# Two blocks on one core: a weight unit's low part made on GpSimd or on the vector engine

## The chip, the cores and the metric

The kernel runs on one core of a Trainium2 chip. Of the core's engines it uses TensorE (PE in the profile; its weight loads are PEld), the vector engine (DVE), ScalarE (ACT), GpSimd (POOL) and the DMA queues, most of them issued by SyncE (SP). The metric is the device time of one execution in microseconds (us). Three runs of the kernel before the change gave 1938.38, 1938.04 and 1938.17 us, median 1938.17. One more execution was profiled: it took 1938.33 us, and its profile spans 1936.6 us.

## What is computed

Activations of 256 tokens by 1024 features pass through two blocks, each of two layers. A layer is a feed-forward part, a mixer and a second feed-forward part, all with residual additions:

```
x = x + 0.5 * norm(swiglu(norm(x), w_gu, w_down))
x = x + norm(mixer(norm(x)))
x = x + 0.5 * norm(swiglu(norm(x), w_gu, w_down))
```

In the first block the mixer joins three paths: a gated linear recurrence with a short causal convolution of four taps, a chunked state-space path with such a convolution too, and a gated spatial unit. In the second block the mixer is a retention and a latent attention. All is float32, and nearly all of the arithmetic is products of the activations with weight matrices that are read from HBM once: 341 MB go through the main DMA queue.

## The kernel before, in words

**Products in three passes.** A float32 product is made from rounded parts. Each operand is split into a high part in the fast matmul format (`fp32r`) and a low part, the rest. `mm3` issues three matmuls into one accumulator: high by high, high activation by low weight, low activation by high weight. The 256 tokens are two tiles (t = 0 and 1) of 128, and each weight is used by both.

**Weight units.** `_plan` cuts all weights into 658 units of 128 rows by up to 1024 columns in the order of their use. Three processes prepare them: `loader` issues a DMA from SP into one of 6 `raw` buffers; `split_hi` makes the high part `whi` (a cast on DVE or ACT) into one of 9 buffers; `split_lo` makes the low part `wlo` = raw - high into one of 9 buffers (line 702), then gives the raw buffer back and tells the matmuls that the unit is ready. Units whose rows are scaled by a gain (line 704) take another operation. A unit's high and low buffers come free when both tiles have used it.

**The order.** Nothing of the order is written by hand. `program` is a set of processes (generators) that yield one engine operation after another. The class `Sched` runs them on a model of the engines, in which `Engine.make` (line 323) gives each operation a duration, and takes at each step the most urgent of those that could begin first; the urgency is the length of the chain of work behind a step, from the last of six trials, plus a table of constants. `Either` (line 291) holds one operation in two forms for two engines, and `choose` (line 454) takes the engine on which it would end first in the model, with 0.3 us against DVE. The instructions are then issued in that order on each engine, and on the chip semaphores alone hold them back: an engine never takes a later instruction first. Where PE has nothing to do in the model, `filler` puts matmuls on a constant tile (`warm`, line 595) there.

**GpSimd before** makes 48 small powers, of one to three columns (`rs`, `rsyo`, `rsyl`, `rsyv`, `rsyb`: reciprocal roots for the norms), masks (`AFFINE_SELECT`), and issues a few DMAs. Every one of its operations counts as 0.85 us in the model (line 347).

**Names that matter.** `acc` and `tmp` are PSUM tiles; `raw`, `whi`, `wlo`, `big`, `scr`, `keep`, `xTh`, `xTl` lie in SBUF. In the first block's mixers the convolutions are the `SCALAR_TENSOR_TENSOR` rows `big<-big,fm` and `big<-scr,fm,big`. Operations recorded by the model's `issue` (line 469) all show L469.

Of the kernel before, what the change touches and what calls it, by code (L numbers as in the profile page):

```python
# [17 lines left out]
ALU = mybir.AluOpType  # L18
# [105 lines left out]
def _width(u):  # L124
    return len(u[0]) * sum(c[3] - c[2] for c in u[1])
# [83 lines left out]
class Blank:  # L209


    def __getattr__(self, name):
        return self
# [94 lines left out]
def size(ap):  # L308
    n = 1
    for d in ap.shape[1:]:  # L310
        n *= d
    return n
# [6 lines left out]
class Engine:  # L319
# [3 lines left out]
    def __getattr__(self, name):  # L323
        f = getattr(self.real, name)

        def make(out, *a, **k):
            n = size(out)
            lat, func = 0.13, None
            if self.key == "PE":
                lat = 0.2  # L330
                if name == "transpose":
                    dur = 0.109
                elif a[0].dtype == F32R:
                    dur = max(0.107, n / 2400.0) + 0.0143
                else:
                    dur = 0.223
            elif self.key == "ACT":
                dur = (0.052 if a[0].space == PSUM else 0.093) + n * 0.000833
                if "accum_out" in k:
                    dur += 0.05  # L340
                for q in ("scale", "bias", "accum_out"):
                    if q in k and not isinstance(k[q], (int, float)):
                        dur += 0.093
                if name == "activation" and a[1] in TABLES:
                    func = a[1]
            elif self.key == "POOL":
                dur, lat = 0.85, 0.25
            else:
                if name in ("tensor_reduce", "bn_stats"):
                    n = size(a[0])  # L350
                dur = 0.07 + n * 0.00104
                if name == "reciprocal":
                    dur = 0.07 + n * 0.00625
                elif name in ("tensor_copy", "tensor_scalar", "tensor_single_scalar") and a[0].space != PSUM:
                    dur = 0.07 + n * 0.00052
                if name in ("scalar_tensor_tensor", "tensor_scalar") and not isinstance(a[1], (int, float)):
                    dur += 0.06
            op = Op(self.key, f, (out,) + a, k, dur, lat, func)
            op.small = self.key == "PE" and (name == "transpose" or a[0].dtype != F32R)
            op.first = name == "transpose" or k.get("start", False)  # L360
            return op

        return make
# [189 lines left out]
def program(S, nc, pool, psp, x, wst, pfm, prow, post, lnp, mats, ret_dec, inv, pos, out):  # L553
    V, A, G, T = Engine("DVE", nc.vector), Engine("ACT", nc.scalar), nc.gpsimd, Engine("PE", nc.tensor)
    R = Engine("POOL", nc.gpsimd)
# [95 lines left out]
    raws, his, los = {}, {}, {}  # L651

    def gain(u):
        name, l, k = u[2]
        return fmc(name, l)[:, k:k + 1]
# [38 lines left out]
    def split_lo():  # L694
        for i, u in enumerate(units):
            yield hi_ev[i]
            yield from S.take(lo_pool, True)
            w = _width(u)
            los[i] = pool.tile([P, 1024], F32R, tag="wlo", name="wlo", bufs=NLO, align_bytes=256)
            h = his[i][:, :w].bitcast(F32)  # L700
            if u[2] is None:
                yield V.tensor_tensor(los[i][:, :w], raws[i][:, :w], h, op=ALU.subtract)
            else:
                yield V.scalar_tensor_tensor(los[i][:, :w], raws[i][:, :w], gain(u), h, op0=ALU.mult, op1=ALU.subtract)
            S.release(raw_pool)
            S.fire(w_ev[i])
# [1015 lines left out]
    S.spawn(loader())  # L1722
    S.spawn(split_hi())
    S.spawn(split_lo())
    ends = [S.spawn(thread(t)) for t in range(2)]
    S.spawn(prologue())
# [75 lines left out]
```

## Time and profile before

| | |
|---|---|
| median of 3 runs | 1938.17 us (1938.04 to 1938.38) |
| profiled execution, its own time | 1938.33 us |
| its span | 1936.6 us |
| PE busy | 1925.4 us (99%), 9247 matmuls |
| DVE busy | 1494.3 us (77%), 2385 instructions |
| of it wlo without a gain | 765.3 us, 638 instructions |
| ACT busy | 626.9 us (32%) |
| POOL busy | 52.9 us (3%), 76 instructions |
| DMA, main queue | 341.26 MB, 54.3% of the 16 engines' span |

The span is the time from the first to the last instruction; 1.7 us of the execution lie around it. Busy time is the time in which at least one instruction of the engine was under way. A row of a timeline reads: start, length, engine, line, operation, output<-inputs, shape, and in brackets the engine's idle time before it with what ended that. "x3" means three instructions in a row. A row's length covers an instruction from start to end, and the next may start before that end, so the difference of two starts is the time that one really takes from its engine.

### The profile page before, as it was taken

How to read it: one execution, taken by the hardware profiler on the slowest of the kernel's cores; microseconds unless marked ns; L12 is line 12 of the kernel's file. 1: busy time of each engine (PE TensorE's matmuls, PEld its weight loads, DVE VectorE, ACT ScalarE, POOL GpSimd, SP SyncE). 2: the span in 40 equal slices, each digit the busy share in tenths (PEclk: the TensorE clock that was granted, in tenths of full speed). 3: DMA queues.
4: the chain of work that ended last, by engine and by line, in shares of the span. 5: the costliest groups of instructions: out<-in, count | busy, mean ns of one | idle time of the engine just before them, and what ended most of it. 6: DMA issues, size and time to landing. Idle time of an engine off the chain costs nothing.

```text
span 1936.6 us, 24594 instructions
## 1 busy us (share of the span) xinstructions
PE 1925.4 (99%) x9247; PEld 1612.1 (83%) x9247; DVE 1494.3 (77%) x2385; ACT 626.9 (32%) x1136; POOL 52.9 (3%) x76
## 2 busy tenths in 40 slices
PE   9999999999999999999999999999999999999999
PEld 7888988888888898888888888888888888888887
DVE  7977898767767799776777779877777777987774
ACT  5211774211321287320232036631022102662220
POOL 1000010000000001000000000000000000000000
PEclk9999999999999999999999999999999999999999
DMA  8555546555655554654655554356565655545572
GB/s 317 179 191 177 166 148 196 195 167 194 224 177 182 180 168 145 199 190 163 208 186 183 185 180 155 125 178 184 180 203 174 184 181 184 159 126 170 178 217 65
DMA packets 98390, 346.89 MB, mean 179 GB/s; under 512 B 11424, under 2 KB 11680, under 8 KB 98272
## 3 DMA queue, kind: packets, MB, share of 16 engines
q1 hardware_dynamic: 97040, 341.26, 54.3%
q0 software_dynamic: 1088, 4.06, 0.6%
q8 instruction: 72, 1.18, 0.3%
q14 instruction: 46, 0.38, 0.1%
q10 hardware_dynamic: 144, 0.00, 0.0%
HBM read 344.24 MB, written 1.05 MB: 178 GB/s over the span
## 4 chain that ended last, share of the span: by engine, by line
PE 96%; ACT 2%; DVE 1%; POOL 0%; issue 0%; POOLq 0%
PE acc L469 89%; PE tmp L469 7%; ACT big L469 1%; ACT L469 1%; POOL rsyo L469 0%; PE tmp L595 0%; DVE wlo L469 0%; DVE x L469 0%; ACT whi L469 0%; DVE whi L469 0%; DVE big L469 0%; DVE scr L469 0%; ACT scr L469 0%; ACT xTh L469 0%; DVE rswo L469 0%
## 5 line engine op out<-in xcount | busy, mean ns | idle before, releaser
L469 DVE TENSOR_TENSOR wlo<-raw,whi 128x1024 fp32r<-128x1024 f32 (+4 forms) x638 | 765.3, 1201 | 56.1 <-ACT whi L469 43.1
L469 PE MATMUL acc<-whi,xTh 128*128 128x512 f32 (+3 forms) x1888 | 745.1, 395 | 0.0
L469 PE MATMUL acc<-wlo,xTh 128*128 128x512 f32 (+3 forms) x1888 | 729.5, 386 | 1.0 <-DVE wlo L469 1.0
L469 PE MATMUL acc<-whi,xTl 128*128 128x512 f32 (+3 forms) x1888 | 730.0, 387 | 0.0
L469 DVE CAST whi<-raw 128x1024 fp32r<-128x1024 f32 (+1 forms) x402 | 278.4, 692 | 260.7 <-PE acc L469 250.7
L469 PE MATMUL acc<-whi,big 128*128 128x512 f32 x1408 | 457.8, 392 | 0.0
L469 PEld LDWEIGHTS acc<-whi,xTl 128*128 128x128 f32 x1888 | 354.6, 188 | 69.7
L469 PEld LDWEIGHTS acc<-wlo,xTh 128*128 128x128 f32 x1888 | 355.4, 188 | 66.1 <-DVE wlo L469 3.7
L469 PEld LDWEIGHTS acc<-whi,xTh 128*128 128x128 f32 x1888 | 355.0, 188 | 63.8 <-ACT big L469 0.4
L469 ACT CAST whi<-raw 128x1024 fp32r<-128x1024 f32 (+4 forms) x236 | 235.1, 1004 | 303.3 <-PE acc L469 283.7
L469 PEld LDWEIGHTS acc<-whi,big 128*128 128x128 f32 x1408 | 264.5, 188 | 54.0
L469 PE MATMUL acc<-wlo,big 128*128 128x512 f32 x704 | 274.7, 390 | 0.0
L469 ACT ACTIVATE scr<-acc,rs 128x512 f32<-128x512 f32 (+3 forms) x123 | 79.9, 650 | 482.0 <-PE acc L469 477.7
L469 PEld LDWEIGHTS acc<-wlo,big 128*128 128x128 f32 x704 | 132.4, 188 | 26.6 <-DVE wlo L469 0.6
L469 DVE SCALAR_TENSOR_TENSOR scr<-acc,rs,scr 128x512 f32<-128x512 f32 (+1 forms) x96 | 67.3, 705 | 42.0 <-PE acc L469 36.1
L469 ACT CAST big<-tmp 128x512 fp32r<-128x512 f32 (+1 forms) x88 | 47.4, 546 | 158.2 <-PE tmp L469 157.8
L469 PE MATMUL tmp<-ident,scr 128*128 128x128 f32 x484 | 78.4, 273 | 0.1
L469 PEld LDWEIGHTS tmp<-ident,scr 128*128 128x128 f32 x484 | 59.9, 140 | 17.2 <-DVE scr L469 2.9
L469 DVE SCALAR_TENSOR_TENSOR xTl<-tmp,fm,xTh 128x128 fp32r<-128x128 f32 x192 | 58.0, 344 | 13.8 <-ACT xTh L469 12.3
L469 ACT ACTIVATE scr<-acc 128x512 f32<-128x512 f32 x24 | 14.2, 596 | 167.2 <-DVE scr L469 167.2
L469 ACT ACTIVATE xTh<-tmp,fm 128x128 fp32r<-128x128 f32 x167 | 53.3, 365 | 44.9 <-DVE xTl L469 23.7
L469 DVE TENSOR_TENSOR big<-tmp,big 128x512 fp32r<-128x512 f32 (+2 forms) x104 | 64.2, 633 | 3.5 <-ACT big L469 2.8
(222 smaller groups left out, 946.0 us busy)
## 6 DMA issues: line engine op xcount, KB each, us to landing
raw<-in_wst_dram SPq DMA_DIRECT2D x606, 512.0 KB, 3.6
raw<-in_wst_dram SPq DMA_DIRECT2D x28, 384.0 KB, 3.1
raw<-in_wst_dram SPq DMA_DIRECT2D x8, 416.0 KB, 3.1
raw<-in_wst_dram SPq DMA_DIRECT2D x8, 390.0 KB, 3.2
pg<-in_post_dram POOLq DMA_DIRECT2D x5, 512.0 KB, 3.9
raw<-in_wst_dram SPq DMA_DIRECT2D x8, 256.0 KB, 4.7
x<-in_x_dram SPq DMA_DIRECT2D x4, 256.0 KB, 4.9
out_dram<-x SPq DMA_DIRECT2D x4, 256.0 KB, 2.0
```

The costliest lines, as they stand in the source:

```text
L469: op.f(*op.a, **op.k)
```

## The change

`split_lo` may now take the low part of a unit without gain on either engine: the same subtraction is offered on DVE and on GpSimd, and `choose` picks one. The model's duration of a GpSimd operation of four columns or more becomes 0.1 us + 0.0019 us a column (768 columns count as 1.56 us and 1024 as 2.05 us); smaller ones keep 0.85 us.

```diff
@@ Engine.make
             elif self.key == "POOL":
-                dur, lat = 0.85, 0.25
+                dur, lat = 0.85 if n < 4 else 0.1 + n * 0.0019, 0.25
@@ split_lo
             if u[2] is None:
-                yield V.tensor_tensor(los[i][:, :w], raws[i][:, :w], h, op=ALU.subtract)
+                yield Either(*(e.tensor_tensor(los[i][:, :w], raws[i][:, :w], h, op=ALU.subtract) for e in (V, R)))
```

In the new order 61 of the 658 low parts are made on POOL, 36 of them 1024 columns wide, 21 of 768 or 780 and 4 of 512. Four are among the first six units of the program, 17 lie in the mixer of the first block's first layer and 18 in that of its second, and 22 are spread over the rest. As the model's times differ, the order changes on all engines. Of the filler matmuls on PE, 57 of 256 columns become 39, and 2 of 128 columns become 10.

**POOL in the first layer's mixer.** `rsyo`, `rs`, `rsyv` and `rsyb` are the small powers, the last number before the arrow tells them apart; `pg` is a DMA of gains. Before:

```order
L469 TENSOR_TENSOR rs_0_1677<-rsw_0_1762,mhalf 128x1
L469 TENSOR_TENSOR rsyo_1_1865<-rswo_1_1863,mhalf 128x1
L469 TENSOR_TENSOR rs_1_1840<-rsw_1_1905,mhalf 128x1
L469 TENSOR_TENSOR rsyv_0_2434<-rswv_0_2432,mhalf 128x1
L902 DMA pg<-in_post_dram 128x1024
L469 TENSOR_TENSOR rsyv_1_2578<-rswv_1_2576,mhalf 128x1
L469 TENSOR_TENSOR rsyb_0_2748<-rswb_0_2746,mhalf 128x1
L469 TENSOR_TENSOR rsyb_1_2876<-rswb_1_2874,mhalf 128x1
```

The same place now:

```order
L469 TENSOR_TENSOR rs_1_1840<-rsw_1_1907,mhalf 128x1
L469 TENSOR_TENSOR wlo<-raw,whi 128x780 x2
L469 TENSOR_TENSOR wlo<-raw,whi 128x768 x2
L469 TENSOR_TENSOR wlo<-raw,whi 128x1024 x3
L469 TENSOR_TENSOR wlo<-raw,whi 128x768 x4
L469 TENSOR_TENSOR wlo<-raw,whi 128x1024
L469 TENSOR_TENSOR rsyv_0_2484<-rswv_0_2482,mhalf 128x1
L469 TENSOR_TENSOR wlo<-raw,whi 128x1024
L902 DMA pg<-in_post_dram 128x1024
L469 TENSOR_TENSOR wlo<-raw,whi 128x1024 x2
L469 TENSOR_TENSOR rsyv_1_2714<-rswv_1_2712,mhalf 128x1
L469 TENSOR_TENSOR rsyb_0_2682<-rswb_0_2680,mhalf 128x1
```

Fifteen subtractions now stand between the powers (two more, of 768 and 780 columns, stand a little ahead), and a power behind one of them waits for it.

**DVE at the convolutions of the same mixer.** Before:

```order
L469 SCALAR_TENSOR_TENSOR big_1679<-big_1679,fm 128x128 x7
L469 TENSOR_TENSOR wlo<-raw,whi 128x780
L469 SCALAR_TENSOR_TENSOR big_1679<-big_1679,fm 128x128 x7
L469 TENSOR_TENSOR wlo<-raw,whi 128x768
L469 SCALAR_TENSOR_TENSOR big_1679<-big_1679,fm 128x128 x7
L469 TENSOR_TENSOR wlo<-raw,whi 128x768 x2
L469 COPY big_1842<-keep 128x7x3
L469 TENSOR_SCALAR big_1842<-big_1842,fm 128x128 x4
L469 TENSOR_TENSOR wlo<-raw,whi 128x768
```

The same place now:

```order
L469 SCALAR_TENSOR_TENSOR big_1667<-big_1667,fm 128x128 x7
L469 CAST whi<-raw 128x768
L469 SCALAR_TENSOR_TENSOR big_1667<-big_1667,fm 128x128 x7
L469 TENSOR_TENSOR wlo<-raw,whi 128x768
L469 SCALAR_TENSOR_TENSOR big_1667<-big_1667,fm 128x128 x7
L469 TENSOR_TENSOR wlo<-raw,whi 128x768
L469 SCALAR_TENSOR_TENSOR dt_0_2101<-acc_1924,rs_0_1665,rows 128x6
```

Subtractions have left DVE, a cast has come to it from ACT, and the rows of the state-space path (`dt`) have moved up.

**POOL at the start of the program.** Now:

```order
masks.py:199 AFFINE_SELECT ident<-ident 128x128
L469 TENSOR_TENSOR wlo<-raw,whi 128x512 x4
L469 TENSOR_TENSOR rs_0_99<-rsw_0_249,mhalf 128x1
L469 TENSOR_TENSOR rs_1_105<-rsw_1_350,mhalf 128x1
L959 MEMSET U 128x128
```

Before, the first `rs` followed the `AFFINE_SELECT` at once; the first two units' low parts, which DVE made, are among the four.

## Rows read from the trace of the kernel before

**Rows 1.** The page: span, and busy time, share and instructions of each engine.

```profile
span 1936.6 us, 24594 instructions
PE 1925.4 (99%) x9247; PEld 1612.1 (83%) x9247; DVE 1494.3 (77%) x2385; ACT 626.9 (32%) x1136; POOL 52.9 (3%) x76
```

**Rows 2.** Windows: stretch, length, busy us (instructions) by engine, PE clock, DMA share, GB/s.

```profile
212.00:275.00 63.00, 61.31 (x374) 56.77 (x373) 62.73 (x199) 58.14 (x105) 2.31 (x4) 1.00 0.45 150
320.00:400.00 80.00, 80.00 (x368) 66.12 (x367) 56.71 (x61) 17.59 (x23) 0.00 (x0) 1.00 0.56 187
689.00:752.00 63.00, 61.33 (x374) 56.78 (x373) 62.74 (x198) 58.15 (x104) 2.41 (x4) 1.00 0.44 149
```

**Rows 3.** Timeline of PE, the end of the first layer's mixer.

```profile
266.17 0.71 PE L595 MATMUL tmp<-warm 128*128 128x256 bf16 x5
...
267.63 0.66 PE L469 MATMUL tmp<-ident,big 128*128 128x128 f32 x4 [0.64 <-DVE big L469]
...
269.49 0.66 PE L469 MATMUL tmp<-big 128*128 128x128 f32 x4
269.99 0.61 PE L469 MATMUL tmp<-big,keep 128*128 128x128 f32 x4
271.64 0.55 PE L469 MATMUL tmp<-ident,big 128*128 128x128 f32 x3 [1.04 <-ACT big L469]
...
273.15 0.48 PE L469 MATMUL acc<-whi,xTh 128*128 128x512 f32 x1
```

**Rows 4.** Timeline of PE, the first product of the program.

```profile
7.05 0.48 PE L469 MATMUL acc<-whi,xTh 128*128 128x512 f32 x1
8.06 0.50 PE L469 MATMUL acc<-wlo,xTh 128*128 128x512 f32 x1 [0.52 <-DVE wlo L469]
8.39 0.40 PE L469 MATMUL acc<-whi,xTl 128*128 128x512 f32 x1
```

**Rows 5.** Windows of the mixer, instructions on tile wlo alone: PE, PEld, DVE.

```profile
212.00:275.00 63.00, 27.54 (x79) 14.70 (x78) 18.11 (x17) 1.00 0.45 150
```

**Rows 6.** DVE groups by shape, 212 to 275 us: count, busy us, mean ns.

```profile
L469 DVE TENSOR_TENSOR wlo<-raw,whi 128x1024 fp32r<-128x1024 f32 x8 | 9.7, 1212 | 0.0
L469 DVE TENSOR_TENSOR wlo<-raw,whi 128x768 fp32r<-128x768 f32 x8 | 7.4, 942 | 0.0
```

**Rows 7.** Timeline of DVE at the convolutions.

```profile
217.44 0.95 DVE L469 TENSOR_TENSOR wlo<-raw,whi 128x768 fp32r<-128x768 f32 x1
218.31 1.93 DVE L469 SCALAR_TENSOR_TENSOR big<-big,fm 128x128 f32<-128x128 f32 x7
```

**Rows 8.** Timeline of POOL.

```profile
25.13 4.34 POOL L469 TENSOR_TENSOR rs<-rsw,mhalf 128x1 f32<-128x1 f32 x1 [7.55 <-DVE rsw L469]
...
29.70 0.29 POOL L960 TENSOR_SCALAR_AFFINE_SELECT U<-U 128x128 f32<-128x128 f32 x1
...
30.22 1.01 POOL L963 TENSOR_SCALAR_AFFINE_SELECT SL<-SL 128x128 f32<-128x128 f32 x1
...
187.40 0.55 POOL L469 TENSOR_TENSOR rsyo<-rswo,mhalf 128x1 f32<-128x1 f32 x1 [82.70 <-DVE rswo L469]
```

**Rows 9.** Timeline of DVE beside the first two of these.

```profile
24.97 2.35 DVE L469 TENSOR_TENSOR wlo<-raw,whi 128x1024 fp32r<-128x1024 f32 x2
27.24 0.68 DVE L469 CAST whi<-raw 128x1024 fp32r<-128x1024 f32 x1
27.84 1.22 DVE L469 TENSOR_TENSOR wlo<-raw,whi 128x1024 fp32r<-128x1024 f32 x1
29.06 0.75 DVE L469 SCALAR_TENSOR_TENSOR scr<-acc,rs,scr 128x512 f32<-128x512 f32 x1
```

**Rows 10.** Timeline of DVE between 29.85 and 30.2 us.

```profile
29.73 1.35 DVE L469 TENSOR_TENSOR wlo<-raw,whi 128x1024 fp32r<-128x1024 f32 x1
```

**Rows 11.** Windows of the mixer, tile tmp alone: PE, PEld, DVE, ACT.

```profile
212.00:275.00 63.00, 17.70 (x139) 14.75 (x123) 8.92 (x31) 9.23 (x28) 1.00 0.45 150
```

**Rows 12.** Windows of the mixer, tile acc alone: PE, PEld, DVE, ACT.

```profile
212.00:275.00 63.00, 47.89 (x235) 41.12 (x234) 0.41 (x2) 6.15 (x10) 1.00 0.45 150
```

## The prediction

> **What bounds the kernel now.** I read the page first. PE is busy for 1925.4 of 1936.6 us [rows 1], so the span is PE's own work with little air in it, and no relief of another engine can give back more than PE loses by waiting. DVE, from which the change takes work, is busy 77% of the span. That is an average over two kinds of stage, and the windows part them [rows 2]. In the second row, a feed-forward stretch, PE is busy for all of 80 us and DVE for 56.7 of them: DVE waits there, and taking work from it is worth nothing. In the first and third rows, the mixers of the first block's two layers, DVE is busy for 62.7 of 63 us, and PE is idle for 1.7 us. There DVE sets the pace.
>
> How much PE loses in such a mixer is read from its timeline [rows 3]. The stretch from the first filler at 266.17 to the return of full products at 273.15 is 6.98 us long. It holds 28 small matmuls, and four of them in a row take 0.50 us from start to start (269.49 to 269.99), so their work is 28 x 0.125 = 3.5 us. The other 3.5 us are waits, on DVE and on ACT by the brackets, and fillers that were put into waits. The second mixer has the same busy times [rows 2], so the two lose 7.0 us. The third place where DVE holds PE is the first product [rows 4]: 1.01 us lie between the starts at 7.05 and 8.06, where the next pair are 0.33 us apart; about 0.8 us is the wait for the low part. **All that the change can win is therefore 7.0 + 0.8 = 7.8 us**, 0.4% of the kernel.
>
> **What leaves DVE.** In the window of the first mixer DVE makes 17 low parts in 18.1 us [rows 5], of 1.21 us at 1024 columns and 0.94 us at 768 [rows 6]. What one really takes is the distance to the next start: 217.44 to 218.31, 0.87 us for 768 columns [rows 7], 0.08 less than its length. With the same 0.08 off, 1024 columns take 1.13 us. The change moves 17 units of this mixer, 7 of them 1024 wide and 10 of 768 or 780: 7 x 1.13 + 10 x 0.87 = 16.6 us freed. The second mixer moves one more of 768 columns, and I price both alike.
>
> **What they cost on GpSimd.** No row shows a subtraction of that width on POOL. The lower bound is DVE's own 1.21 us. For the upper one, a mask of 128 columns took 0.29 us at 29.70 [rows 8]; eight of them would be 2.3 us. I take 2.0 us, nearer the upper end, because that mask is the only row with a wide input on POOL, and it reads one input where the subtraction reads two. The 17 units have 14,884 columns, or 14.5 times 1024, so POOL works on them for 29 us; the ends are 17.6 and 33.4 us. GPSIMD Engine Reference of the Trainium skill, section 3.1, gives 4497 ns for an addition of 2048 float32 columns; half of it, 2.25 us, is an estimate by that page, with which this sum would be 32.7 us, and no run so far shows it.
>
> **Whether the two engines run side by side.** This decides the sign. A power on POOL takes 0.55 us at 187.40 [rows 8]. At 25.13 the same operation on one column took 4.34 us, until 29.47. Beside it DVE ran three low parts and a cast without a gap, all between SBUF tiles, and then, at 29.06, an operation that reads an accumulator in PSUM [rows 9]. The power ended 0.41 us after that start. So it stood still as long as DVE worked between SBUF tiles, and was let through at the first DVE operation that did not. The reverse shows too: the mask at 29.70 and a low part on DVE that began 0.03 us later ran together, and the low part took 1.35 us [rows 10] instead of 1.21 [rows 6]. The mask at 30.22 then took 1.01 us, with that low part still under way to 31.08. I read this as one way into SBUF that the two engines take in turns. SBUF — State Buffer of the Trainium skill, section "SBUF: two separate sides", states it as a rule against this change: GpSimd and a DVE operation with two SBUF inputs, or in its two-port mode, hold a shared pair of ports in turn, each for a whole instruction. The row at 25.13 agrees as far as POOL's waiting goes; that DVE is kept out for the whole of a wide POOL operation no row here shows.
>
> How much of DVE's other work in the mixer would have to wait? Of its 62.73 us [rows 2], 18.1 are low parts, 8.92 touch tmp [rows 11] and 0.41 touch acc [rows 12], the PSUM tiles. The rest is 35.3 us, which is 79% of the 44.6 us that are not low parts. If POOL holds the way in for its 29 us, DVE is kept from work for 0.79 x 29 = 23 us, against 16.6 us freed: **DVE is 6.4 us later per mixer, not earlier**. At the ends it is 0.79 x 17.6 - 16.6 = -2.7 us and 0.79 x 33.4 - 16.6 = +9.8 us.
>
> **What reaches PE.** Between nothing and all of it. For 54 of the 63 us DVE was full and PE had no wait, as weights were made ahead; at the end of the mixer the brackets name DVE and ACT at once [rows 3]. I take half, 3.2 us a mixer, 6.4 us for both. The start wins the 0.8 us of rows 4, if POOL makes the first low part while DVE goes on with the activations; there the DVE work that competes is short. The 22 subtractions elsewhere cost nothing: the feed-forward row, with 23 us of 80 free on DVE [rows 2], is their cover. If it failed, each would hold PE for at most the 2.3 - 1.13 = 1.2 us by which POOL is slower, 26 us in all; that DVE had 23 us free makes a small part of this the most that I expect, and it lies within the range. The DMAs on POOL's queue (`pg`) are issued a stage ahead of their use. Eighteen fewer wide fillers on PE and eight more narrow ones are air that was counted above. The casts that move between ACT and DVE follow from the new order, and I price them at nothing: ACT is busy 32% [rows 1].
>
> **Sum.** On the profiled execution's 1938.33 us (its span is 1936.6; the median of the three runs is 1938.17, 0.2 us less): +6.4 - 0.8 = +5.6 us, about 1944. With none of the delay on PE it is 1937.5; with the upper end all on PE it is 1938.3 + 19.6 - 0.8 = 1957.
>
> **Rivals.** About 0.2%, 3.9 us, is what a measurement of this kernel can tell from no change.
> First, **relief**: the engines mostly run side by side, DVE is freed of 16.6 us a mixer, and PE's waits in rows 3 close. It then gains up to 7.8 us, 1930.5; half of that is 1934.4. For it speaks that the mask and the low part at 29.70 did overlap with only 0.14 us of delay; against it the 4.34 us. It decides if a wide POOL operation delays DVE by less than 16.6 / (0.79 x 14.5) = 1.45 us per 1024 columns, which is possible only near the lower bound of its length. Chance 0.18.
> Second, **hidden**: units made ahead absorb POOL's slowness and the time freed on DVE is used up by the blocking; 1938, within 4 us. For it speaks that PE ran without a wait until 266.17 beside a full DVE [rows 2, 3], and that what is freed and what is blocked, 16.6 and 23 us, lie close together. Chance 0.20.
> Third, **POOL starves**: DVE keeps the way in through its convolutions (seven operations back to back between low parts, rows 7), and POOL's row waits as at 25.13, 4.34 - 0.55 = 3.8 us for each. In the new order four low parts of the narrow projections stand in a line on POOL; 4 x 3.8 = 15 us late, and PE takes its matmuls in the order given, so it stops on `wlo`. The powers `rsyv` and `rsyb` behind such rows are late too. If half is covered by units made ahead, that is 7.6 us a mixer and 1938.3 + 15.2 - 0.8 = 1953; it decides where the wait exceeds what the unit was ahead by. Chance 0.17.
> That the change moves nothing is ruled out by the order: 61 subtractions stand on POOL.
>
> **How the numbers follow.** The forecast, taking turns, has 0.45, the rivals 0.18, 0.20 and 0.17. The forecast is 1944 with a range of its own from 1938 to 1952 (none of the delay on PE to all of 2 x 6.4 us, and a little over). The range that should hold the time 8 times in 10 reaches from 1931, the relief in full, to 1957, the upper end in full. Faster by over 0.2% is the relief without its weakest part: 0.18. Within 0.2% are the hidden case and the forecast's lower edge: 0.20 + 0.07 = 0.27. Slower is 0.38 + 0.17 = 0.55.
>
> **What would show it.** Right: wide subtractions on POOL of 2 us and more, some of 3 to 5 us where DVE runs between SBUF tiles; on DVE, low parts and convolution rows that take longer than 1.21 and 0.27 us beside them; PE idle in the mixers above 1.7 us in 63, with `DVE big` or `POOL wlo` in the brackets. Wrong: POOL subtractions of one length wherever they stand, DVE rows as long as before, and no waits of PE in the windows of the mixers. The start would be wrong if PE still waited about 0.8 us for the first low part.

## The result, and the profile after

The change makes the kernel slower: 2005.6 us (median of 4 runs, 2003.17 to 2007.35) against 1938.11 us, a ratio of 1.0347 with a 95% interval of 1.0332 to 1.0362. The prediction had 1944 us, slower, and at most 1957. The sign is right, and POOL does hold DVE as forecast; the size is off by a factor of twelve: +67.5 us where +5.6 was forecast. The profiled execution took 2003.17 us.

The page of the changed kernel, to be read against [rows 1]:

```profile
span 2001.4 us, 24609 instructions
PE 1946.1 (97%) x9237; PEld 1622.7 (81%) x9237; DVE 1539.8 (77%) x2376; ACT 605.2 (30%) x1088; POOL 188.9 (9%) x137
```

PE is idle for 2001.4 - 1946.1 = 55.3 us, where it was idle for 11.2 us: 44.1 us more. It is also busy for 20.7 us longer, with ten matmuls fewer. Together these are the 64.8 us by which the span grew. DVE is busy 45 us longer, although it has lost 61 subtractions. Part of that is work that the new order moved to it from ACT: 2385 - 61 would be 2324 instructions, DVE has 2376, and ACT has 48 fewer than before. The rest is the first sign of what happened: its other instructions became longer. Experiment 5 below, with the same order and nothing wide on POOL, has DVE busy for 1459.8 us, 80.0 less than here.

Windows (stretch, length, busy us and instructions of PE, PEld, DVE, ACT, POOL, then PE clock, DMA share, GB/s): the two mixers of the first block, a feed-forward stretch, and in the last row ten microseconds of the first mixer. They answer to [rows 2].

```profile
212.00:287.00 75.00, 60.01 (x324) 54.52 (x322) 73.15 (x177) 48.59 (x83) 34.18 (x17) 0.89 0.41 132
330.00:410.00 80.00, 80.00 (x370) 66.05 (x369) 56.83 (x71) 17.95 (x26) 3.48 (x3) 1.00 0.52 174
700.00:775.00 75.00, 62.44 (x341) 57.24 (x339) 66.33 (x171) 47.12 (x91) 30.35 (x18) 0.91 0.40 131
245.00:255.00 10.00, 2.55 (x11) 2.46 (x12) 10.00 (x34) 5.73 (x10) 4.48 (x3) 0.54 0.30 102
```

The feed-forward stretch is as full as before. In the mixers PE, idle for 1.7 us in 63 before, is idle for 15.0 and 12.6 us in 75. The other places are the mixers of the second block:

```profile
1200.00:1290.00 90.00, 87.26 (x486) 75.63 (x484) 80.86 (x187) 47.70 (x105) 7.08 (x5) 0.98 0.46 145
1700.00:1830.00 130.00, 122.87 (x663) 104.50 (x662) 110.48 (x228) 64.52 (x131) 14.67 (x8) 0.97 0.43 132
```

The groups of the subtractions on POOL, by shape (count, busy us, mean ns, idle time before them):

```profile
L469 POOL TENSOR_TENSOR wlo<-raw,whi 128x1024 fp32r<-128x1024 f32 x36 | 90.6, 2525 | 402.6 <-DVE whi L469 291.4 <-ACT whi L469 65.2 <-DVE scr L469 19.9
L469 POOL TENSOR_TENSOR wlo<-raw,whi 128x768 fp32r<-128x768 f32 x15 | 30.8, 2060 | 33.2 <-ACT whi L469 19.8 <-DVE whi L469 6.5 <-PE tmp L469 4.5
```

What stands beside one of them on DVE? First the timeline of POOL, then that of DVE, at the convolutions of the first mixer:

```profile
233.92 7.23 POOL L469 TENSOR_TENSOR wlo<-raw,whi 128x1024 fp32r<-128x1024 f32 x3 [6.99 <-issue]
248.10 3.67 POOL L469 TENSOR_TENSOR wlo<-raw,whi 128x768 fp32r<-128x768 f32 x2 [6.95 <-ACT whi L469]
```

```profile
233.70 8.39 DVE L469 SCALAR_TENSOR_TENSOR big<-big,fm 128x128 f32<-128x128 f32 x7
242.08 1.92 DVE L469 SCALAR_TENSOR_TENSOR big<-big,fm 128x128 f32<-128x128 f32 x7
248.22 1.89 DVE L469 SCALAR_TENSOR_TENSOR big<-scr,fm,big 128x128 f32<-128x128 f32 x1
250.03 1.76 DVE L469 SCALAR_TENSOR_TENSOR spp<-spp,spq 128x6 f32<-128x6 f32 x1
251.79 0.60 DVE L469 TENSOR_SCALAR scr<-acc,rs 128x384 f32<-128x384 f32 x1
```

Seven convolution rows take 8.39 us beside POOL's three subtractions, since three of the seven each wait for one. Seven of the same take 1.92 us when POOL rests, as in [rows 7]. It is not a matter of size: at 250.03 an operation on six columns takes 1.76 us. Over the kernel the groups of DVE say which operations suffer:

```profile
L469 DVE SCALAR_TENSOR_TENSOR big<-big,fm 128x128 f32<-128x128 f32 x84 | 42.2, 571 | 0.0
L469 DVE SCALAR_TENSOR_TENSOR xTl<-tmp,fm,xTh 128x128 fp32r<-128x128 f32 x192 | 57.9, 343 | 23.1 <-ACT xTh L469 20.7 <-PE acc L469 2.0
L469 DVE SCALAR_TENSOR_TENSOR spp<-spp,spq 128x6 f32<-128x6 f32 x28 | 7.6, 273 | 0.3
```

The first and the third work between SBUF tiles; before, they took 344 and 159 ns. The second has the same shape as the first and reads `tmp`, in PSUM: 344 ns before, 343 now, though over 20 of them started under a subtraction.

And PE? Its timeline, and its waits (us in total, times, longest):

```profile
242.61 0.39 PE L469 MATMUL acc<-wlo,xTh 128*128 128x512 f32 x1
242.84 0.40 PE L469 MATMUL acc<-whi,xTl 128*128 128x512 f32 x1
252.45 0.90 PE L469 MATMUL tmp<-ident,scr 128*128 128x128 f32 x3 [9.21 <-DVE scr L469]
...
254.86 0.63 PE L469 MATMUL acc<-wlo,xTh 128*128 128x512 f32 x1
255.28 0.63 PE L469 MATMUL acc<-whi,xTl 128*128 128x512 f32 x1
```

```profile
PE tmp L469 <- DVE scr L469: 29.9, 7, 9.2
PE acc L469 <- DVE xTl L469: 8.2, 4, 2.5
PE acc L469 <- DVE wlo L469: 0.8, 3, 0.4
```

PE stands for 9.21 us at one transpose, until DVE has made `scr` (the row at 251.79). DVE is busy in all of that time; it is simply late. This stop and its twin of 9.19 us in the second layer are PE's two longest. In the kernel before, ACT made all eight `scr` of this form (`scr<-acc,rs`, 128x384); the new order gave two of them to DVE, and these are the two at which PE stops. No wait of PE names POOL. Windows of the time around that stop:

```profile
236.00:242.80 6.80, 6.80 (x40) 6.59 (x39) 6.80 (x10) 3.56 (x5) 5.15 (x3) 1.00 0.52 160
252.40:256.10 3.70, 3.65 (x14) 3.36 (x15) 3.70 (x13) 2.56 (x6) 1.86 (x2) 0.50 0.47 163
256.10:258.00 1.90, 1.90 (x16) 1.76 (x15) 1.90 (x4) 1.63 (x5) 1.81 (x1) 1.00 0.49 134
```

For 3.7 us after the stop PE is granted half its clock (0.50, the lower of its two levels), though it is busy. The trace has nine stretches at 0.50, 47.7 us together, and PE is busy for 34.5 us of them. In the rows above, two matmuls of 512 columns start 0.42 us apart at 0.50 (254.86, 255.28) and 0.23 at 1.00 (242.61, 242.84). By that the work of the 34.5 us would take about 16 us less at the full clock (an estimate), so most of the 20.7 us of longer busy time lie there.

### The profile page after: what moved, and what is told of

It reads as the page before. It is cut to its first block, busy times and chain, and to the rows that moved or that the text cites. A ratio compares the mean times of both kernels' runs of the same rounds, so it can differ in the third digit from the quotient of the medians.

```text
span 2001.4 us, 24609 instructions
## 1 busy us (share of the span) xinstructions
PE 1946.1 (97%) x9237; PEld 1622.7 (81%) x9237; DVE 1539.8 (77%) x2376; ACT 605.2 (30%) x1088; POOL 188.9 (9%) x137
## 4 chain that ended last, share of the span: by engine, by line
PE 81%; DVE 11%; issue 5%; ACT 2%; DMA 0%; POOL 0%; SPq 0%; DVEq 0%; ACTq 0%; POOLq 0%
PE acc L469 75%; PE tmp L469 6%; DVE big L469 5%; DVE scr L469 2%; DVE wlo L469 1%; DVE whi L469 1%; ACT big L469 0%; DVE x L469 0%; ACT whi L469 0%; DMA keep<-in_mats_dram 0%; PE tmp L595 0%; DVE xTl L469 0%; ACT scr L469 0%; ACT L469 0%; DVE keep L469 0%
## 5 line engine op out<-in xcount | busy, mean ns | idle before, releaser
L469 PE MATMUL acc<-whi,xTh 128*128 128x512 f32 (+2 forms) x1888 | 748.7, 397 | 2.6 <-DVE rswv L469 2.6
L469 PE MATMUL acc<-whi,xTl 128*128 128x512 f32 (+2 forms) x1888 | 733.2, 388 | 8.2 <-DVE xTl L469 8.2
L469 DVE TENSOR_TENSOR wlo<-raw,whi 128x1024 fp32r<-128x1024 f32 (+3 forms) x577 | 700.4, 1215 | 48.4 <-ACT whi L469 35.4
L469 PE MATMUL acc<-wlo,xTh 128*128 128x512 f32 (+2 forms) x1888 | 732.8, 388 | 0.8 <-DVE wlo L469 0.8
L469 DVE CAST whi<-raw 128x1024 fp32r<-128x1024 f32 (+2 forms) x425 | 296.0, 697 | 284.9 <-PE acc L469 277.0
L469 ACT CAST whi<-raw 128x1024 fp32r<-128x1024 f32 (+4 forms) x213 | 213.6, 1009 | 275.6 <-PE acc L469 250.2
L469 POOL TENSOR_TENSOR wlo<-raw,whi 128x1024 fp32r<-128x1024 f32 (+3 forms) x61 | 137.8, 2264 | 459.1 <-DVE whi L469 303.1
L469 DVE SCALAR_TENSOR_TENSOR scr<-acc,rs,scr 128x512 f32<-128x512 f32 x96 | 67.4, 704 | 33.5 <-PE acc L469 28.4
L469 POOL TENSOR_TENSOR rs<-rsw,mhalf 128x1 f32<-128x1 f32 x24 | 21.5, 895 | 662.9 <-DVE rsw L469 490.2
L469 DVE SCALAR_TENSOR_TENSOR xTl<-tmp,fm,xTh 128x128 fp32r<-128x128 f32 x192 | 57.9, 343 | 23.1 <-ACT xTh L469 20.7
```

What stands on the lines that cost most here:

```text
L469: op.f(*op.a, **op.k)
```

## The experiments

Two theories stood against each other. **Hold**: while a wide instruction runs on POOL, DVE stands at its first operation between SBUF tiles, and all behind it in its row stands too; PE waits for DVE. **Order**: the new order, laid out with other durations, is bad by itself. A third, **late**, was that PE waits for low parts that POOL makes late. All differences below are against 1938.1 us.

**1. The new order without POOL.** The subtraction is offered on both engines, so the order is the same, but both offers issue to DVE.

```diff
+ops = [e.tensor_tensor(los[i][:, :w], raws[i][:, :w], h, op=ALU.subtract) for e in (V, R)]
+ops[1].f = ops[0].f
+yield Either(*ops)
```

> The order of the changed kernel on every engine, but all low parts are issued to DVE: nothing of the 61 subtractions runs on POOL. If POOL's way into SBUF is the cause (while a wide POOL subtraction runs, DVE is held at its first operation that needs SBUF, and all behind it in DVE's row waits too), the time returns to that of the kernel before: 1938 to 1950, since the order was made for other lengths and DVE has its 16.6 us per mixer back to do. If the new order by itself is bad (planned with a low part on POOL that never delays DVE), it stays near 2000. A time between, 1960 to 1985, would divide the loss.

Measured: 1968.59 us, ratio 1.0158 (1.0143 to 1.0173), +30.5 us, between the two. PE stops at the same transpose, for 3.87 us instead of 9.21:

```profile
241.91 0.90 PE L469 MATMUL tmp<-ident,scr 128*128 128x128 f32 x3 [3.87 <-DVE scr L469]
```

So the order costs something when DVE has to make the low parts after all. This kernel alone can't tell whether that is the order's fault or DVE's, as DVE now has 61 subtractions that the order did not reckon with, and besides them the work that the order took from ACT: 52 instructions more than in the kernel before, and 1517.5 us busy against 1494.3.

```profile
PE 1939.0 (99%) x9237; PEld 1616.6 (82%) x9237; DVE 1517.5 (77%) x2437; ACT 604.6 (31%) x1088; POOL 48.3 (2%) x76
```

**2. POOL without the new order.** The order of before; the 61 units that went to POOL are issued to POOL where DVE stood.

```diff
+ON_POOL = {...}
...
+op = V.tensor_tensor(los[i][:, :w], raws[i][:, :w], h, op=ALU.subtract)
+if i in ON_POOL:
+    op.f = nc.gpsimd.tensor_tensor
+yield op
```

> The order of the kernel before, in which the same 61 units' low parts are issued to POOL where DVE stood. If POOL's subtractions hold DVE, the loss is there without the new order: 1985 to 2015, with DVE rows that end about 0.1 us after POOL's. If the new order is the cause, 1938 to 1945. If PE waits because POOL's low parts are late (2.4 us for 1.2), the time is above 1938 too, but PE's waits name POOL and its tile wlo rather than DVE.

Measured: 1989.94 us, 1.0267 (1.0252 to 1.0282), +51.8 us. POOL alone does most of the damage. Here POOL's own lateness shows as well: DVE waits 14.7 us for the power `rsyo` that stands behind subtractions in POOL's row (6.5 us before), and PE 2.4 us for `wlo` from POOL:

```profile
PE tmp L472 <- ACT scr L472: 17.1, 3, 8.3
PE acc L472 <- POOL wlo L472: 2.4, 3, 1.1
```

The first of these lines is the hold again, by way of ACT: in the first mixer ACT had stood for 8.72 us at an input that DVE makes behind its held convolutions.

The timelines of POOL and then of DVE in its first mixer show the hold in both directions:

```profile
216.47 10.89 POOL L472 TENSOR_TENSOR wlo<-raw,whi 128x780 fp32r<-128x780 f32 x3 [2.43 <-issue]
230.61 12.20 POOL L472 TENSOR_TENSOR wlo<-raw,whi 128x1024 fp32r<-128x1024 f32 x5 [3.25 <-ACT whi L472]
```

```profile
215.59 5.59 DVE L472 SCALAR_TENSOR_TENSOR big<-big,fm 128x128 f32<-128x128 f32 x21
225.84 0.18 DVE L472 COPY big<-keep 128x21 f32<-128x21 f32 x1 [3.80 <-ACT big L472]
231.98 11.25 DVE L472 SCALAR_TENSOR_TENSOR big<-big,fm 128x128 f32<-128x128 f32 x6
```

At 215.59 DVE runs 21 convolution rows at full pace, and POOL's three subtractions take 10.89 us, some 5 more than alone: here DVE keeps POOL out. At 231.98 six such rows take 11.25 us beside five subtractions: one row of DVE to one of POOL. What decides which of the two happens was not tried. Between them DVE stands for 3.80 us, waiting for ACT. Over the mixer the windows, first of this kernel and then of the kernel before, show where the freed time went:

```profile
200.00:287.00 87.00, 75.72 (x424) 69.38 (x422) 70.20 (x196) 63.18 (x119) 40.89 (x20) 0.92 0.39 130
```

```profile
200.00:287.00 87.00, 85.31 (x509) 78.29 (x508) 81.38 (x234) 68.44 (x128) 4.49 (x7) 1.00 0.45 149
```

DVE is idle for 16.8 of 87 us, where it was idle for 5.6. It got its time back in places where its inputs weren't there yet, and was held in others.

**3. Outside the mixers only.** The choice is offered to units outside the four mixers; it sends 22 to POOL.

```diff
+mixer = any(m <= i < n for m, n in MIXERS)
...
+yield ops[0] if mixer else Either(*ops)
```

> Only the units outside the four mixers may go to POOL, by the same choice; 22 subtractions do. The prediction priced them at nothing: 1936 to 1942, all of the loss being in the mixers. If each POOL subtraction costs PE about 1 us wherever it stands (67.5 us / 61), 1960. At the start the prediction wanted 0.8 us less than before; the trace of the changed kernel shows no gain there, so none is expected.

Measured: 1955.7 us, 1.0090 (1.0075 to 1.0105), +17.6 us. The expectation was wrong. Part of the loss lies right behind the mixers, where DVE is still catching up:

```profile
275.00:310.00 35.00, 31.05 (x153) 23.91 (x152) 33.10 (x54) 17.59 (x37) 13.46 (x8) 1.00 0.54 180
```

PE is idle for 3.95 of these 35 us (0.13 in the same window before), and DVE is busy for 33.1. "Outside the mixers" by unit number is not outside them in time. The same place in the second layer loses as much, so the two make some 7.6 of the 16.4 us by which the span grew. Another 9.1 us are longer busy time of PE (1934.5 us against 1925.4), at a mean granted clock of 0.999 and with 56 more fillers, all of them at the end of the first block's mixers. That air stands in the new order itself; no run made this order without POOL, so how much of the loss is the order's stays open.

**4. Work on POOL that nothing waits for.** The kernel before, DVE makes all low parts; behind 61 of them POOL subtracts once more, into the raw tile that is dead by then.

```diff
 yield V.tensor_tensor(los[i][:, :w], raws[i][:, :w], h, op=ALU.subtract)
+if i in ON_POOL:
+    nc.gpsimd.tensor_tensor(raws[i][:, :w], raws[i][:, :w], h, op=ALU.subtract)
...
```

> The kernel before, with all low parts on DVE as they were; behind the low part of each of the same 61 units POOL subtracts once more, into the raw tile that nobody reads any more (added work that no result needs; a raw buffer comes free some 2.4 us later). PE can't wait for it. If POOL's mere use of SBUF holds DVE, the time rises although nothing depends on the result, and by more than in the changed kernel, since DVE keeps its own low parts: 61 x about 2.3 us = 140 us of POOL time, of which the two mixers of the first block and those of the second have 39 units or 80 to 90 us: 2010 to 2040. If only lateness of the low parts counts, or the order, it stays at 1938 to 1941.

Measured: 2031.07 us, 1.0478 (1.0460 to 1.0495), +93.0 us. Nobody needs these results, so late low parts can't be the cause; the order is that of before, so the order can't be either. One lateness is left: the small powers stand behind the added work in POOL's row, and DVE waits 16.8 us for `rsyo`, where it waited 6.5. These 10.3 us are a small part of the 93.0; PE's waits for `x`, which DVE makes behind `rsyo`, grow from 1.2 to 12.0 us, and in them both causes meet.

```profile
DVE x L472 <- POOL rsyo L472: 16.8, 11, 3.1
```

The timelines of POOL and of DVE show one row of operations with POOL beside it and the same without:

```profile
254.22 2.48 POOL L707 TENSOR_TENSOR raw<-raw,whi 128x1024 f32<-128x1024 f32 x1 [3.40 <-DVE big L472]
```

```profile
253.88 2.96 DVE L472 SCALAR_TENSOR_TENSOR big<-scr,fm,big 128x128 f32<-128x128 f32 x3
256.89 0.86 DVE L472 SCALAR_TENSOR_TENSOR big<-scr,fm,big 128x128 f32<-128x128 f32 x3
```

The hold is shown: 2.10 us on DVE for 2.48 us of POOL.

**5. The new order with DVE relieved and POOL idle.** The order of the changed kernel, row by row, but what it gives to POOL isn't made; PE multiplies by the unit's high part in its place.

```diff
...
+ops[1].f = lambda *_, **__: los.update({i: his[i]})
...
```

> The order of the changed kernel on every engine, row by row, but the 61 low parts that it gives to POOL are made by nobody: PE multiplies by the unit's high part once more in their place (this changes the result). DVE is relieved as the order was planned for, POOL has nothing to hold DVE with. If the loss of 67 us is POOL's hold on DVE, the time is at or a little below that of the kernel before: 1930 to 1942. If the order is bad even with DVE relieved, 1955 and more, with PE's long waits on DVE's scr at about 240 and 740 us as in the changed kernel.

Measured: 1933.53 us, 0.9977 (0.9967 to 0.9986), -4.6 us. Its page, and windows of its two first mixers, against [rows 1] and [rows 2]:

```profile
PE 1923.7 (100%) x9237; PEld 1607.9 (83%) x9237; DVE 1459.8 (76%) x2376; ACT 603.0 (31%) x1088; POOL 47.1 (2%) x76
```

```profile
212.00:275.00 63.00, 62.89 (x378) 58.05 (x377) 59.14 (x204) 54.57 (x93) 3.26 (x4) 1.00 0.56 182
689.00:752.00 63.00, 62.88 (x386) 58.26 (x386) 59.04 (x198) 52.39 (x89) 3.13 (x4) 1.00 0.54 176
```

The order is good, a little better than the old one, if DVE really has the time that the order reckons with. PE's waits in the mixers fall from 1.7 to 0.1 us. DVE is busy for 34.5 us less than in the kernel before: subtractions of 61.4 us have left it, and work of ACT's has come to it. From here to the changed kernel nothing in the order differs, only the subtractions on POOL come in: they cost 72.1 us. Against this run the 61 subtractions put back on DVE (experiment 1) cost 35.1 us, for 61.4 us of DVE's time (36 x 1.13 + 21 x 0.87 + 4 x 0.60; the last is a 512-column row by the same rule).

**6. One partition of 128.** As 4, but on a 128th of the data.

```diff
-    nc.gpsimd.tensor_tensor(raws[i][:, :w], raws[i][:, :w], h, op=ALU.subtract)
+    nc.gpsimd.tensor_tensor(raws[i][:1, :w], raws[i][:1, :w], h[:1], op=ALU.subtract)
```

> As the idle work on POOL that cost 93 us, but each of the 61 added subtractions works on one partition of the 128, over the same columns: 1/128 of the data, for what should be about the same time on POOL. If POOL holds DVE for the whole of an instruction, whatever it moves, the time is as there, 2010 to 2035. If it is the traffic that collides, 1938 to 1942.

Measured: 2031.06 us, 1.0482 (1.0466 to 1.0497): the same time as with all partitions. The groups on POOL of experiments 4 and 6:

```profile
L707 POOL TENSOR_TENSOR raw<-raw,whi 128x1024 f32<-128x1024 f32 x36 | 89.9, 2498 | 701.5 <-DVE wlo L472 607.6 <-issue 42.7 <-DVE rsyh L472 17.8
```

```profile
L707 POOL TENSOR_TENSOR raw<-raw,whi 1x1024 f32<-1x1024 f32 x36 | 89.6, 2489 | 701.5 <-DVE wlo L472 525.7 <-DMA raw<-in_wst_dram 82.0 <-issue 42.7
```

It is not traffic that collides. An instruction holds the way in for as long as it runs, whatever it moves.

**7. A copy instead of a subtraction.** As 4, with one input.

```diff
-    nc.gpsimd.tensor_tensor(raws[i][:, :w], raws[i][:, :w], h, op=ALU.subtract)
+    nc.gpsimd.tensor_copy(raws[i][:, :w], h)
```

> As the idle work on POOL that cost 93 us, but each of the 61 added instructions is a copy of the unit's high part into the dead raw tile: one input where the subtraction has two. The mask with one input took 0.29 us for 128 columns, so some 1 to 2.3 us at 1024. If every wide POOL instruction holds DVE, the loss goes with its length: 93 us times its length over the subtraction's 2.4. If only one with two inputs does, 1938 to 1943.

Measured: 1961.20 us, 1.0119 (1.0104 to 1.0135), +23.1 us. The copy takes less than half as long, and it holds DVE too:

```profile
L707 POOL COPY raw<-whi 128x1024 f32<-128x1024 f32 x36 | 41.9, 1165 | 706.5 <-DVE wlo L472 549.0 <-DMA raw<-in_wst_dram 82.2 <-issue 31.6
```

By its length the loss would have been 93.0 x 1.165 / 2.5 = 43 us. It is about half of that. By the table below DVE was held for 0.40 of the copies' time and for 0.64 of the subtractions'; why a copy holds it for a smaller share was not tried.

**8. Seventeen units outside the mixers, old order.** As 2, with those of the 61 that lie outside.

> The order of the kernel before, with only the 17 units outside the four mixers, of the 61, issued to POOL. The prediction priced such ones at nothing: 1936 to 1942. With the loss of 51.7 us for all 61 spread evenly, 14 us: 1952. I expect 1940 to 1948, since some of them stand right behind a mixer, where DVE is still late.

Measured: 1940.39 us, 1.0012 (1.0002 to 1.0021), +2.3 us, 0.14 us a unit. If the two parts simply add up, 49.5 of the 51.8 us of experiment 2 belong to the 44 units in mixers.

**9. The subtractions in pieces.** The changed kernel, 128 columns an instruction.

```diff
...
+for c in range(0, o.shape[-1], 128):
+    e = min(c + 128, o.shape[-1])
+    nc.gpsimd.tensor_tensor(o[:, c:e], r[:, c:e], h[:, c:e], op=op)
...
```

> The changed kernel with each of the 61 subtractions on POOL cut into pieces of 128 columns (436 in all). The mask of 128 columns took 0.29 us, so a unit's eight pieces take about 2.4 us, as before. If POOL keeps DVE out from the first column of an instruction to its last, DVE now gets in after each piece: the longest DVE rows shrink from 2.5 to some 0.6 us and the time falls, to 1950 to 1990. If DVE is kept out until POOL's row of instructions is empty, or the pieces cost as much in their own overhead, 2000 and more.

Measured: 1984.81 us, 1.0245 (1.0228 to 1.0263), +46.7 us, a third less than the change itself. POOL and DVE at the convolutions:

```profile
238.06 2.80 POOL L705 TENSOR_TENSOR wlo<-raw,whi 128x128 fp32r<-128x128 f32 x6
238.18 1.48 DVE L469 SCALAR_TENSOR_TENSOR big<-big,fm 128x128 f32<-128x128 f32 x3
```

The two now alternate, piece by operation: a start every 0.47 us on either engine, where DVE alone starts a convolution row every 0.27 (1.92 us for seven). Here the turn is taken per instruction.

**10. A plan that knows of the hold.** POOL's duration is set to the measured one, and DVE is counted as taken while POOL subtracts.

```diff
-dur, lat = 0.85 if n < 4 else 0.1 + n * 0.0019, 0.25
+dur, lat = 0.85 if n < 4 else 0.1 + n * 0.00225, 0.25
...
+if op.key == "POOL" and op.dur > 0.9:
+    self.free["DVE"] = max(self.free["DVE"], s + op.dur)
```

> The changed kernel, planned with POOL's measured length (2.4 us per 1024 columns instead of 2.05) and with DVE counted as held for as long as a wide subtraction runs on POOL; the choice itself is made as before and still puts 50 subtractions on POOL. If PE's loss is DVE's lateness against an order that trusted it to be early, an order made with the hold loses less than 67 us: 1950 to 1985. If it is the hold itself, however it is planned, 1990 to 2010. Below 1938 is expected by neither: the time freed on DVE was worth 4.6 us and each unit still holds it longer than its low part took.

Measured: 1998.40 us, 1.0313 (1.0298 to 1.0329), +60.3 us, with 50 subtractions on POOL. That is 1.21 us a unit, against 1.11 in the changed kernel. Knowing the hold did not help the order. The choice of the engine still went by POOL's own length alone, and no other choice was tried; this order too has no run without POOL.

**All runs in one table.** DVE's hold is worked out from the traces: for each DVE instruction that overlaps one of the wide POOL instructions (in experiment 9, one of the pieces), its length less the median length of the same operation in the kernel before, summed where that is over 0.05 us. POOL's time is the sum of the lengths.

| kernel | wide on POOL | POOL us | DVE held, us | time, us |
|---|---|---|---|---|
| the change | 61 | 138.1 | 83.1 | +67.5 |
| 1 new order, all on DVE | 0 | 0 | 0 | +30.5 |
| 2 old order, POOL | 61 | 147.9 | 63.0 | +51.8 |
| 3 outside mixers, replanned | 22 | 54.7 | 19.2 | +17.6 |
| 4 idle work | 61 | 136.9 | 88.0 | +93.0 |
| 5 new order, none made | 0 | 0 | 0 | -4.6 |
| 6 idle, one partition | 61 | 136.5 | 88.0 | +93.0 |
| 7 idle copy | 61 | 65.1 | 26.2 | +23.1 |
| 8 outside mixers, old order | 17 | 37.9 | 8.6 | +2.3 |
| 9 in pieces of 128 columns | 436 pieces | 257.2 | 56.7 | +46.7 |
| 10 plan knows | 50 | 116.4 | 73.3 | +60.3 |

Wherever POOL worked in the mixers or just behind them, the kernel lost 0.8 to 1.1 us for each microsecond that DVE was held, whether DVE had been freed of the low parts (2, 9, 10, the change) or not (4, 6, 7). Experiment 8, outside, lost 0.27. These ratios hold the relief too in all but 4, 6 and 7, and another order in 3, 9, 10 and the change. For the order of the change experiment 5 is the run without POOL, and against that the ratio is 72.1 / 83.1 = 0.87; the orders of 3 and 10 have no such run.

No version here beats both kernels. In this order the most there was to win is what experiment 5 shows, 4.6 us, with low parts that cost nothing.

## Why the prediction was right in kind and wrong in size

- **DVE sets the pace in the mixers, and little can be won: right.** The ceiling was 7.8 us. With 61 low parts left out the kernel won 4.6.
- **The start: the wait went, the gain did not come.** By rows 4 the wait was 1.01 - 0.33 = 0.68 us, a little under the 0.8 of the sum. In experiment 5 the first product runs without a pause, and PE then stands 0.80 us for the next activations: a transfer is late there instead.

```profile
6.69 0.71 PE L469 MATMUL acc<-whi,xTh 128*128 128x512 f32 x2
8.57 0.66 PE L469 MATMUL tmp<-ident,x 128*128 128x128 f32 x4 [0.80 <-DMA x<-in_x_dram]
```

- **A subtraction on POOL, 2.0 us: too low.** The rows that no DVE operation delayed take 2.37 to 2.41 us at 1024 columns and 1.82 to 1.88 at 768 and 780. The upper bound, 2.3, was itself too low; it was eight masks, and a mask has one input. The estimate of 2.25 us from GPSIMD Engine Reference of the Trainium skill, section 3.1, was nearer than 2.0, and a little low too. In the first mixer (205 to 300 us) POOL took 35.4 us for 16 units, in the second (697 to 800) 39.4 for 18, against the 29 forecast for 17.
- **One way into SBUF, in turns: right, and now shown** by experiments 4, 6 and 9. The rule of SBUF — State Buffer in the Trainium skill, section "SBUF: two separate sides", is that one engine has the shared pair of ports for a whole instruction, and the other blocks. The 1.76 us of six columns at 250.03 agree with it. At 216.47 in experiment 2 POOL waits for 21 instructions of DVE and not for one, and what lets it in or keeps it out stays open. PE's waits name `DVE scr` (29.9 us) most, where `DVE big` or `POOL wlo` was expected.
- **The blocked share, 0.79: right.** DVE was held for 28.5 of POOL's 35.4 us in the first mixer (0.81) and for 28.4 of 39.4 in the second (0.72), by the sum of the table. Forecast were 23 us each: the share was right, POOL's time too low.
- **POOL starves: not in the changed kernel.** It was a rival at 0.17. POOL's longest subtraction took 4.45 us, only three took over 3 us, and PE waited for no low part from POOL. In the old order it does happen, at 216.47 in experiment 2: PE waits 2.4 us for low parts there, and DVE's waits for `rsyo` grow by 8.2, of a loss of 51.8 us.
- **"23 us blocked - 16.6 freed = +6.4 us per mixer", and of that "half" to PE: this step failed.** It set one against the other as if a microsecond freed and a microsecond held were worth the same. The runs price them apart. Freed: 61.4 us of subtractions left DVE, its busy time fell by 34.5, and the kernel won 4.6 us (experiment 5), since PE had hardly anything to wait for. Held: 83.1 us cost 72.1 on top of that. In the profiles of these two kernels, whose spans differ by 69.4 us, 47.0 of them are idle time of PE and 22.4 its longer busy time. So 0.57 of the hold came to PE as waiting, not far from the half that was assumed, but of the whole hold and not of a small difference. PE's longer busy time adds the rest.
- **Two things kept the freed time from standing against the hold.** In the new order it was spent in advance. PE's row is laid out for a DVE that has it, and DVE's row was filled up with work of ACT's, a move that the prediction priced at nothing. With that work and all low parts on DVE, and none on POOL, experiment 1 loses 30.5 us; how much of this is the layout and how much the 23.2 us of added work was not separated. In the old order the freed time went by unused: in experiment 2 DVE was freed of 61.4 us and held for 63.0, as good as nothing in the difference, and the kernel lost 51.8 us, while DVE's idle time in the mixer trebled. Time freed in one place can't be saved up for the place where DVE is held. With the hold priced in full, from the prediction's own numbers, two mixers held for 23 us each would have been 46 us less a gain of at most 7.8, about 1976. Of the 83.1 us that were measured, 26.2 lie outside the two mixers, where the sum had nothing.
- **"The 22 subtractions elsewhere cost nothing": wrong as to place.** By unit number 44 of the 61 belong to the four mixers, and the other 17 cost 2.3 us together in the old order (experiment 8). But units that are made just behind a mixer, and those in the second block's mixers, hold DVE where PE waits for it. In the second block PE of the changed kernel is idle for 2.7 of 90 and 7.1 of 130 us, in the same windows of the kernel before for 0.0 and 0.4. Experiment 3 lost 17.6 us with another 22 in another order, and PE's idle time behind the first block's mixers is some 7.6 of that.
- **The clock was not in the sum at all.** 20.7 us of the loss are PE's longer busy time, and by the estimate above about 16 of them come from a granted clock of 0.50 after stops such as that at 243.24.

The upper end of the range, 1957, took the net delay with all of it on PE. The cost that was really unknown, what PE pays for a DVE that is late against its order, had as its upper end the whole hold, and the range left that out.

## What to carry to other kernels

Don't net relief against delay. Time taken off a helper engine is worth no more than the bound engine's waits, which the profile shows; time by which the helper is held has no such ceiling. Here the kernel paid 0.8 to 1.1 us for each microsecond of it in the mixers, in an order planned for the relief and in one that wasn't. When an order is made by a program, count also the work that it moves onto the relieved engine. Before wide work between SBUF tiles goes to GpSimd beside a full vector engine, one run with idle work of that kind (experiment 4) shows without any change of the order that there is a price, though not its size: 93.0 us there, 67.5 in the change. A plan that gives GpSimd a row of its own must take the vector engine's time for it too; the one plan here that did still lost 60.3 us (experiment 10).

## What the runs showed of the hardware that was not expected

- A POOL subtraction over one partition takes as long as over 128 (2489 and 2498 ns at 1024 columns) and holds DVE as long: 2031.06 and 2031.07 us.
- A copy on POOL, with one input, holds DVE too, but takes 1165 ns where the subtraction takes 2498.
- Not every DVE operation between SBUF tiles is held. In experiment 4 two `RECIPROCAL` of six columns take their usual 0.24 us in the midst of POOL's first subtraction, and the subtraction on DVE right behind them takes 2.40 instead of 0.94. POOL, then DVE:

```profile
262.95 5.04 POOL L707 TENSOR_TENSOR raw<-raw,whi 128x768 f32<-128x768 f32 x2 [1.58 <-DVE scr L472]
```

```profile
263.73 0.24 DVE L472 RECIPROCAL spz<-spz 128x6 f32<-128x6 f32 x2
263.89 2.40 DVE L472 TENSOR_TENSOR wlo<-raw,whi 128x768 fp32r<-128x768 f32 x1
```

- A DVE operation on six columns can take 1.76 us instead of 0.16. One that reads PSUM is not held, even when a second operand lies in SBUF (`xTl<-tmp,fm,xTh`: 343 ns with and 344 without POOL at work).
- After a stop of 9.21 us PE ran for 3.7 us at a granted clock of 0.50, though its row was full again.
